# A decoder layer on one core: earlier fronts, reused tiles and one operand layout in an RWKV recurrence, and four residual adds moved through PSUM

## The chip, the cores and the metric

The kernel runs as one program on one core of a Trainium2 chip. The metric is the device time of one execution in microseconds (us). All tensors are float32.

## The reference, cut to what matters

One layer of a trunk, sequence 1024, width 1024. One projection of the normalised input feeds three things: an RWKV-7 branch, an S5 branch and two gates. The branches are gated, merged, projected and added to the input; a gated feed-forward block follows.

```python
def step(S, inp):                       # per head, 64x64 state
    r_t, w_t, k_t, v_t, a_t, b_t = inp  # a = -kk, b = kk * sigmoid(..)
    sa = jnp.einsum('bhij,bhj->bhi', S, a_t)
    S = S * w_t[:, :, None, :] + sa[..., None] * b_t[:, :, None, :] \
        + v_t[..., None] * k_t[:, :, None, :]
    return S, jnp.einsum('bhij,bhj->bhi', S, r_t)
y = group_norm(y) * lnx_w + lnx_b       # over each head
y = (y + sum(r * k * r_k) * v) * g
mixed = (g_rwkv * o_rwkv + g_s5 * o_s5) @ w_out
x = x + rms_norm(mixed, norm_mix_post)
x = x + rms_norm(conv_ffn(rms_norm(x, norm_ffn_pre)), norm_ffn_post)
```

## The kernel before, in words

Data lies with channels on the partitions and 512 time steps (a half, `th`) in a row. A product of float32 operands is made of three matmuls of split operands (high by high, low by high, high by low), at L179, L180 and L181 in the first half of the program; their outputs are the tiles `gm`, `ch` and so on. Weights are loaded by SP into `wf` (two buffers), cast to a high part `wh` by ACT (L159) and a low part `wl` by DVE (L160), four buffers each.

**The recurrence** is cut into four groups i = 0 to 3: a group is four heads (`g` = i % 2, as two pairs u = 0 and 1 of two heads on 128 partitions) over one half of the time (`th` = i // 2). A group goes through these functions:

- `rwkv_front` (L679), once per pair: loads k, tz, ta and r into tiles `ld` (ten buffers, L696), makes the norm of k with matmuls (L706), an inverse square root on DVE, a scan (L712), exponentials on ACT (L716, L717), the operands `ar` (L723, L732) and `bk` (L724, L735), and the products G of the two (L746), masked by DVE (L748) into `gr`. L727 copies the norm into `yb` for the transposes L729.
- `rwkv_inv` (L792): 62 small DVE operations (L805, L807) that invert triangles, fed and read back through DRAM by POOL.
- `rwkv_nat` (L764): transposes. `rwkv_level` (L819): joins the inverse's blocks with 32x32 matmuls (L832, L834) and ACT copies (L833, L835).
- `rwkv_chain` (L847): eight dependent chunks of 64 time steps that carry the state S, each with matmuls L880, L862, L891, L893, L898, L903 and, between them, short DVE and ACT operations (L883, L894, L895, L905, L866).
- `rwkv_out` (L917): group norm (L936 to L946), transposes (L952), scale and bias on ACT (L954), and two DVE operations (L957) with `bv` and `TG`, loaded through SP; the result goes to DRAM (`YR`).

**The order** of the instructions is written when the program is built, by `drive` (L203). It keeps an estimated clock `now` and runs generators ("lanes"): the chain lane (L2013), which takes the groups in order through nat, out of the group before, level and chain; two preparation lanes (L1991), one per pair, for front and inverse; and one for the S5 gate. When no lane is ready, it emits a step of the "fill": the gate products, the S5 products and the merge, independent work of three matmuls a piece. A lane gives with each `yield` how long it is not to be called again: T_KN after the front's first part, T_BK before G, T_INV for the inverse, T_LN for the norm. These constants, and conditions on counters, set where everything stands in each engine's queue. A queue is worked off in order on the chip.

In the preparation lane the front of group i may start once `nat` of group i - 1 is out. While it stands before `merge_s5`'s gates and the fourth chain is not done (`pause`), no fill is emitted.

**The end**: after the last product of the down projection, a sum of squares (`sumsq`, L263), an inverse root, a broadcast (`spread`, L289), and for eight tiles y = f * gain * bc (L1794) and y + residual (`add`, L1702), both on DVE, then one DMA each through SP (L1796).

## Time and profile before

| | |
|---|---|
| Median of 3 runs | 1569.41 us (1565.72 to 1578.88) |
| The profiled execution's own time | 1572.7 us |
| Its span | 1570.7 us |
| Mean granted TensorE clock | 0.964 of full speed |
| PE busy | 1488.5 us (95%) |
| DVE busy | 1164.0 us (74%) |
| ACT busy | 732.1 us (47%) |
| DMA | 224.46 MB, 143 GB/s |

The page's second part cuts the span in 40 slices of 39.3 us; a digit is the busy share in tenths, and PEclk is the clock that TensorE was granted. PE's busy time is not all useful: at a lower clock the same matmul is busy for longer, so that a stretch is read by busy time and clock together. The recurrence lies between about 275 and 814 us.

### The profile page before, as it was taken

The numbers are of one execution on the slowest core, as the hardware profiler recorded it, in microseconds if no ns is written. First come the engines' busy times: TensorE is split into PE (matmuls) and PEld (weight loads), VectorE is DVE, ScalarE is ACT, GpSimd is POOL, SyncE is SP. The second block draws the span as 40 slices with busy tenths as digits, with TensorE's granted clock in tenths as the row PEclk, the third lists the DMA queues.
The fourth block names the chain that finished last, engine by engine and source line by source line (L and its number), as shares of the span: only waits on it lengthen the run. The fifth ranks groups of instructions, "written<-read, shape, count | busy, mean of one in ns | idle before, by whom it ended". The sixth has DMA issues, their size and how long they took to land. (4 is left out here: it accounts for less than half of the span.)

```text
span 1570.7 us, 23456 instructions
## 1 busy us (share of the span) xinstructions
PE 1488.5 (95%) x8606; PEld 1193.9 (76%) x8606; DVE 1164.0 (74%) x2132; ACT 732.1 (47%) x1206; POOL 181.4 (12%) x340
## 2 busy tenths in 40 slices
PE   7997999999999989799799999999999999999995
PEld 5786888878676667577578788788888887788784
DVE  8878975747365569786467869788888887698777
ACT  6354434332344365257534556455555555443451
POOL 0022110123221121303100011000000000000000
PEclk9998999999998999899789999999999999999997
DMA  6454344443333174425325676233333335943722
GB/s 212 122 149 130 97 139 127 155 134 102 104 118 122 55 252 150 128 75 177 120 81 187 203 246 203 95 121 111 111 110 111 121 114 201 333 163 121 241 68 107
DMA packets 121123, 224.46 MB, mean 143 GB/s; under 512 B 30976, under 2 KB 37120, under 8 KB 121008
## 3 DMA queue, kind: packets, MB, share of 16 engines
q1 hardware_dynamic: 90144, 154.02, 30.9%
q0 software_dynamic: 21024, 64.71, 12.3%
q10 hardware_dynamic: 9840, 4.24, 1.0%
q8 instruction: 67, 1.10, 0.3%
q14 instruction: 48, 0.39, 0.1%
HBM read 163.41 MB, written 57.41 MB: 141 GB/s over the span
## 5 line engine op out<-in xcount | busy, mean ns | idle before, releaser
L179 PE MATMUL gm<-hh,wh 128*128 128x512 f32 x688 | 289.6, 421 | 6.9 <-ACT hh L244 6.2
L180 PE MATMUL gm<-hl,wh 128*128 128x512 f32 x688 | 273.7, 398 | 2.7 <-DVE hl L245 2.6
L181 PE MATMUL gm<-hh,wl 128*128 128x512 f32 x688 | 272.5, 396 | 0.0
L159 ACT CAST wh<-wf 128x512 fp32r<-128x512 f32 x178 | 109.9, 620 | 182.0 <-PE gm L180 111.6
L160 DVE TENSOR_TENSOR wl<-wf,wh 128x512 fp32r<-128x512 f32 x178 | 122.8, 693 | 73.1 <-ACT wh L159 71.9
L179 PEld LDWEIGHTS gm<-hh,wh 128*128 128x128 f32 x688 | 131.4, 191 | 41.3 <-ACT hh L244 9.1
L180 PEld LDWEIGHTS gm<-hl,wh 128*128 128x128 f32 x688 | 131.9, 192 | 28.8 <-DVE hl L245 6.2
L181 PEld LDWEIGHTS gm<-hh,wl 128*128 128x128 f32 x688 | 131.5, 191 | 28.6
L1751 PE MATMUL d<-xl,wh 128*128 128x512 f32 x308 | 120.5, 391 | 4.9 <-DVE xl L245 4.9
L1750 PE MATMUL d<-xh,wh 128*128 128x512 f32 x308 | 120.3, 391 | 0.3 <-DVE p L1702 0.3
L1752 PE MATMUL d<-xh,wl 128*128 128x512 f32 x308 | 119.9, 389 | 0.0
L1573 PE MATMUL rp<-t,h 128*128 128x512 f32 x252 | 98.3, 390 | 2.1 <-ACT p L1587 2.1
L1575 PE MATMUL rp<-t,l 128*128 128x512 f32 x252 | 98.1, 389 | 0.0
L1574 PE MATMUL rp<-t,h 128*128 128x512 f32 x252 | 98.0, 389 | 0.0
L1751 PEld LDWEIGHTS d<-xl,wh 128*128 128x128 f32 x308 | 57.8, 188 | 18.8 <-DVE xl L245 7.1
L244 ACT CAST h<-r 128x1024 fp32r<-128x1024 f32 (+1 forms) x40 | 34.0, 849 | 73.1 <-PE rp L1574 64.3
L1750 PEld LDWEIGHTS d<-xh,wh 128*128 128x128 f32 x308 | 57.8, 188 | 12.9 <-issue 0.7
L245 DVE TENSOR_TENSOR l<-r,h 128x1024 fp32r<-128x1024 f32 (+1 forms) x40 | 38.9, 972 | 38.5 <-ACT h L244 38.5
L1752 PEld LDWEIGHTS d<-xh,wl 128*128 128x128 f32 x308 | 57.8, 188 | 12.0
L1594 DVE SCALAR_TENSOR_TENSOR y<-zv,vecs,y 128x1023 f32<-128x1023 f32 (+1 forms) x42 | 53.8, 1282 | 10.2 <-ACT y L1592 10.2
L1573 PEld LDWEIGHTS rp<-t,h 128*128 128x128 f32 x252 | 47.3, 188 | 12.7 <-ACT p L1587 2.9
L1574 PEld LDWEIGHTS rp<-t,h 128*128 128x128 f32 x252 | 47.3, 188 | 9.8
(460 smaller groups left out, 3374.7 us busy)
## 6 DMA issues: line engine op xcount, KB each, us to landing
r<-in_w_up_dram SPq DMA_DIRECT2D x42, 512.0 KB, 3.6
wf<-in_w_in_dram SPq DMA_DIRECT2D x72, 256.0 KB, 3.1
st<-in_w_down_dram SPq DMA_DIRECT2D x55, 256.0 KB, 4.5
st<-ACT SPq DMA_DIRECT2D x44, 256.0 KB, 4.2
ACT<-y POOLq DMA_DIRECT2D x21, 512.0 KB, 2.9
GT<-ev POOLq DMA_DIRECT2D x32, 256.0 KB, 3.5
wf<-in_w_br_dram SPq DMA_DIRECT2D x32, 256.0 KB, 3.4
wf<-in_w_out_dram SPq DMA_DIRECT2D x32, 256.0 KB, 2.9
```

Of the source, the lines that this page charges most:

```text
L159: self.last_wh = nc.scalar.copy(h[:, :n], f[:, :n])
L160: low = nc.vector.tensor_tensor(l[:, :n], f[:, :n], h[:, :n].bitcast(F32), ALU.subtract)
L179: mm(ps, a, xh[k], start=a0, stop=False)
L180: mm(ps, a, xl[k], start=False, stop=False)
L181: mm(ps, b, xh[k], start=False, stop=z0)
L1573: mm(ps, wh[:, c], xh, start=first and k == 0, stop=False, skip_group_check=True)
L1574: mm(ps, wh[:, c], xl, start=False, stop=False, skip_group_check=True)
L1575: mm(ps, wl[:, c], xh, start=False, stop=k == 3, skip_group_check=True)
L1594: V.scalar_tensor_tensor(y[:, lag:], z[:, 0:1024 - lag], self.vec(nme, i), y[:, lag:], ALU.mult, ALU.add)
L1750: mm(ps, wh[:, c], xh[:, x], start=start, stop=False, skip_group_check=True)
L1751: mm(ps, wh[:, c], xl[:, x], start=False, stop=False, skip_group_check=True)
L1752: mm(ps, wl[:, c], xh[:, x], start=False, stop=stop, skip_group_check=True)
```

## The change

1. **Fronts earlier.** A preparation lane starts group i's loads once the chain of group i - 2 is out (`chains`); a second condition, after the wait T_LD, holds the front's other work until `nat` of i - 1 and `out` of i - 2 are out. `ar` and `bk` are allocated there.
2. **Operands alike.** In `ar` both heads of a pair have a in columns 0 to 63 and r in 64 to 127, so that `ar0` and `ar1` are one DVE operation of 128 partitions each where two of 64 were. `tk` lies in `yb` (a part of `gr`) and no longer in a tile `ld`, and the product r * r_k * tk is made in the front's first part.
3. **Outputs in loaded tiles.** `rwkv_out` loads `bv` and `TG` before the wait T_LN, most of them into the chain's spent `ar`; two DVE operations that take scale and bias from vectors replace the ACT operation and the two DVE operations. `rwkv_level` uses the inverse's spare tile `x` where it can.
4. **The planner's constants**: T_KN 17 to 12, T_BK 13 to 10, T_INV 62 to 58.
5. **The end.** The residuals of tiles 4 to 7 go into PSUM by a matmul with the identity (`resid_sum`), two before the sum of squares and two behind it; after L1794's operation a second identity matmul adds y, ACT copies the sum out, and DVE makes only four of the eight adds. The tiles are written in place.

The core of the diff (renamed slices left out):

```diff
     def rwkv_tiles(self, d, g, th):
         d.update(g=g, th=th)
-        pool = self.rk if g else self.rka
-        d["ar"] = self.tg("ar", 1, (128, 2, 8, 128), pool=pool)
-        d["bk"] = self.tg("bk", 1, (128, 2, 8, 128), pool=self.rka)
-        d["gr"] = self.tg("gr", 1, (128, 2, 8, 2, 128), pool=pool)
+        d["gr"] = self.tg("gr", 1, (128, 2, 8, 2, 128), pool=self.rk if g else self.rka)
         d["v"] = {}
         d["pt"] = self.tg("pt", 2, (128, 8, 2))
         d["md"] = self.dram.tile([2, 2, 16, 32, 32], F32, tag="md", name=self.nm("md"), bufs=3)
         d["bv"] = self.dram.tile([2, 128, 512], F32, tag="bv", name=self.nm("bv"), bufs=3)
-    def rwkv_front(self, d, u):
+    def rwkv_operands(self, d):
+        d["ar"] = self.tg("ar", 1, (128, 2, 8, 128), pool=self.rk if d["g"] else self.rka)
+        d["bk"] = self.tg("bk", 1, (128, 2, 8, 128), pool=self.rka)
+
+    def rwkv_front(self, d, u, i):
         nc, V, G, A = self.nc, self.nc.vector, self.nc.gpsimd, self.nc.scalar
         mm = nc.tensor.matmul
         o = slice(d["th"] * 512, d["th"] * 512 + 512)
         p = 2 * d["g"] + u
-        ar, bk = d["ar"][:, u], d["bk"][:, u]
-        ar0, ar1, bk0, bk1 = [[x[HS[h], :, HS[h ^ j]] for h in range(2)] for x in (ar, bk) for j in range(2)]
-
         gf = d["gr"][:, u].rearrange("p c h t -> p (c h t)")
         kk, yb, pe = gf[:, 0:512], gf[:, 512:1024], gf[:, 1024:1544].rearrange("p (c t) -> p c t", t=65)
...
         yield 0, T_LD
+        yield 0, lambda: self.nat >= i - 1 and self.outs >= i - 1
+        if "ar" not in d:
+            self.rwkv_operands(d)
+        ar, bk = d["ar"][:, u], d["bk"][:, u]
+        ar0, ar1 = ar[:, :, 0:64], ar[:, :, 64:128]
+        bk0, bk1 = [[bk[HS[h], :, HS[h ^ j]] for h in range(2)] for j in range(2)]
...
         A.activation(pe[:, :, 1:65], c64(tz), AF.Exp, scale=-0.5 * CDEC)
         A.activation(tz, tz, AF.Exp, scale=0.5 * CDEC)
         G.tensor_copy(d["pt"][:, :, u], pe[:, :, 64])
-        tk = self.tg("ld", NLD)
+        tk = yb
         A.activation(tk, ta, AF.Identity, bias=self.ka_1[:, p:p + 1], scale=self.ka_h[:, p:p + 1])
         V.tensor_tensor(tk, tk, k, ALU.mult)
+        V.tensor_tensor(ar1, c64(r), pe[:, :, 1:65], ALU.mult)
         for h, sl in enumerate(HS):
-            V.tensor_tensor(ar1[h], c64(r)[sl], pe[sl, :, 1:65], ALU.mult)
             V.tensor_tensor(bk1[h], c64(tk)[sl], c64(tz)[sl], ALU.mult)
+        V.scalar_tensor_tensor(r, r, self.vec("r_k", p), tk, ALU.mult, ALU.mult)
         yield 0.9, T_KN, 1.5
         kb = self.rp()
         A.copy(c64(yb), y.unsqueeze(2).to_broadcast([128, 8, 64]))
         for tb in range(4):
             nc.tensor.transpose(kb[:, tb * 128:(tb + 1) * 128], yb[:, tb * 128:(tb + 1) * 128], self.cst("ident"))
         V.scalar_tensor_tensor(kk, k, self.vec("k_k", p), kb, ALU.mult, ALU.mult)
-        for h, sl in enumerate(HS):
-            V.scalar_tensor_tensor(ar0[h], c64(kk)[sl], -1.0, pe[sl, :, 0:64], ALU.mult, ALU.mult)
+        V.scalar_tensor_tensor(ar0, c64(kk), -1.0, pe[:, :, 0:64], ALU.mult, ALU.mult)
         V.scalar_tensor_tensor(kk, ta, 1.0, kk, ALU.add, ALU.mult)
         for h, sl in enumerate(HS):
             V.scalar_tensor_tensor(bk0[h], c64(kk)[sl], 0.5, c64(tz)[sl], ALU.mult, ALU.mult)
         v = ld(self.RKV[8 + p], G)
         yield 0.5, T_BK
-        gm = [self.cst("gmask")[:, x].unsqueeze(1).to_broadcast([128, 4, 128]) for x in (slice(0, 128), slice(64, 192))]
+        gm = self.cst("gmask").unsqueeze(1).to_broadcast([128, 4, 128])
...
         for blk in range(2):
...
-                nc.gpsimd.dma_start(md[h], d["gr"][sl, u, :, h, sl])
-
-        V.scalar_tensor_tensor(r, r, self.vec("r_k", p), tk, ALU.mult, ALU.mult)
+                nc.gpsimd.dma_start(md[h], d["gr"][sl, u, :, h, 32 * blk:32 * blk + 32])
+
         pb = self.rp()
         mm(pb, self.cst("ones_bd"), r, start=True, stop=True)
...
+                    nc.gpsimd.dma_start(d["gr"][sl, u, :, h, 32 * blk:32 * blk + 32], xd[h])
+
...
         p0, p1 = [p0[:, u] for u in range(2)], [self.chb().rearrange("p (c t) -> p c t", t=32) for u in range(2)]
-        xz = self.tg("ld", NLD).rearrange("p (u c t) -> p u c t", u=2, t=32)
+        xz = (self.tg("x", 1, pool=self.rka) if spare else self.tg("ld", NLD)).rearrange("p (u c t) -> p u c t", u=2, t=32)
...
         o = slice(th * 512, th * 512 + 512)
         final = th == 1 and d["g"] == 1
-        ts = []
+        free = d["ar"].rearrange("p u c t -> p (u c t)").rearrange("p (j t) -> p j t", t=512)
         def factors(u):
             r = []
-            for src in (d["bv"][u], self.TG[2 * d["g"] + u][:, o]):
-                t = self.tg("ld", NLD)
+            for j, src in enumerate((d["bv"][u], self.TG[2 * d["g"] + u][:, o])):
+                t = self.tg("ld", NLD) if final or d["g"] > j else free[:, (2 if u == 0 else 0) + j]
                 (G if final else nc.sync).dma_start(t, src)
                 r.append(t)
             return r
         V.tensor_tensor(yn, yn, mean.unsqueeze(2).to_broadcast([128, 16, 64]), ALU.subtract)
         var = self.small.tile([128, 16], F32, tag="lv", name=self.nm("lv"), bufs=2)
         for j in range(2):
-            sq = self.tg("ld", NLD, (128, 8, 64))
+            sq = free[:, j].rearrange("p (a i) -> p a i", i=64)
             A.activation(sq, yn[:, 8 * j:8 * j + 8], AF.Square)
             V.tensor_reduce(var[:, 8 * j:8 * j + 8], sq, AX.X, ALU.add)
         V.tensor_scalar(var, var, 1.0 / 64, 64e-5, ALU.mult, ALU.add)
         y = self.rsqrt(var, 16, "or")
         V.tensor_tensor(yn, yn, y.unsqueeze(2).to_broadcast([128, 16, 64]), ALU.mult)
+        if not final:
+            ts = [factors(u) for u in range(2)]
         yield 0, T_LF if final else T_LN
         for u in range(2):
             p = 2 * d["g"] + u
             ps = self.rp((128, 4, 128))
             for c in range(4):
                 nc.tensor.transpose(ps[:, c], d["yn"][:, c, u], self.cst("ident"))
-            y1 = self.tg("ld", NLD)
-            A.activation(y1, ps.rearrange("p c t -> p (c t)"), AF.Identity, bias=self.vec("lnx_b", p),
-                         scale=self.vec("lnx_w", p))
-            for t, op in zip(ts[u] if final else factors(u), (ALU.add, ALU.mult)):
-                V.tensor_tensor(y1, y1, t, op)
+            y1, tg = ts[u]
+            V.scalar_tensor_tensor(y1, ps.rearrange("p c t -> p (c t)"), self.vec("lnx_w", p), y1, ALU.mult, ALU.add)
+            V.scalar_tensor_tensor(y1, y1, self.vec("lnx_b", p), tg, ALU.add, ALU.mult)
             if final:
                 self.br[p] = self.pair(1, p)
...
                     xs.append(x)
             return xs
-        def outputs(th, src, bc, xs):
+        def outputs(th, src, bc, xs, sums={}):
             for m in OUTORD[th]:
-                y = stage(0)[:, 0:512]
+                y = src[m] if th else stage(0)[:, 0:512]
                 V.scalar_tensor_tensor(y, src[m], self.vec("g_ffn_post", m), bc, ALU.mult, ALU.mult)
-                add(y, y, xs[m])
+                if m in sums:
+                    mm(sums[m], self.cst("ident"), y, start=False, stop=True)
+                    A.copy(y, sums[m])
+                else:
...
-        ss = bank(2)
+        ss, sums = bank(2), {}
+
+        def resid_sum(m, b):
+            sums[m] = bank(b)
+            mm(sums[m], self.cst("ident"), d["xs1"][m], start=True, stop=False)
+        resid_sum(4, 0)
+        resid_sum(5, 1)
         self.sumsq(ss, last[0], True)
         self.sumsq(ss, acc[1], False)
+        for m, b in ((6, 4), (7, 5)):
+            resid_sum(m, b)
         y = self.rstd(ss, 1e-6, 1.0 / D)
         bc = bank(3)
         self.spread(bc, y)
-        outputs(1, f[1], bc, d["xs1"])
+        outputs(1, f[1], bc, d["xs1"], sums)
     def build(self):
...
         for i, d in enumerate(self.ds):
-            yield 0, lambda: self.nat >= i - 1
+            yield 0, lambda: self.chains >= i - 1
             if not d:
                 self.rwkv_tiles(d, i % 2, i // 2)
-            yield from self.rwkv_front(d, u)
+            yield from self.rwkv_front(d, u, i)
             self.fronts += 1
...
             self.leveling = True
-            yield from self.rwkv_level(d)
+            yield from self.rwkv_level(d, i < 3 and self.prep == i)
             self.leveling = False
             yield from self.rwkv_chain(d)
+            self.chains = i + 1
             if i == 3:
                 self.pause, self.chained = False, True
...
 NEVA = 4
-T_KN, T_BK, T_GR, T_INV, T_LV, T_CH, T_LN, T_LF = 17.0, 13.0, 2.5, 62.0, 1.0, 0.8, 16.0, 14.5
```

The change moves the recurrence to other places in the queues. Three places follow.

PE, inside the fourth group's chain (`chk`, `chb` are the chain's PSUM tiles, `gm` those of the fill). Before, the last six chunks follow one another:

```order
L880 MATMUL chk_7890<-S_2603,ar_5878 64x64 x2
L862 MATMUL chk_7890<-UV_7357,gr_5880 64x64 x2
L880 MATMUL chk_7890<-S_2603,ar_5878 64x64 x2
L862 MATMUL chk_7890<-UV_7357,gr_5880 64x64 x2
L891 MATMUL chb_7891<-p_1498_7827,gr_5880 64x64 x4
L893 MATMUL chk_7890<-S_2603,ar_5878 64x64 x4
L898 MATMUL chk_7890<-UV_7357,gr_5880 64x64 x4
L903 MATMUL chb_7891<-UV_7357,bkn_7356 64x64 x4
L880 MATMUL chk_7928<-S_2603,ar_5878 64x64 x2
L862 MATMUL chk_7928<-UV_7357,gr_5880 64x64 x2
```

After, each chunk has six pieces of fill (18 matmuls) between its parts:

```order
L179 MATMUL gm_7470<-hh_6958,wh_7458 128x512
L180 MATMUL gm_7470<-hl_6959,wh_7458 128x512
L181 MATMUL gm_7470<-hh_6958,wl_7459 128x512
L179 MATMUL gm_7470<-hh_7042,wh_7464 128x512
L180 MATMUL gm_7470<-hl_7043,wh_7464 128x512
L181 MATMUL gm_7470<-hh_7042,wl_7465 128x512
L896 MATMUL chb_7493<-p_1388_7429,gr_5590 64x64 x4
L898 MATMUL chk_7492<-S_2603,ar_5731 64x64 x4
L179 MATMUL gm_7470<-hh_7096,wh_7464 128x512
L180 MATMUL gm_7470<-hl_7097,wh_7464 128x512
L181 MATMUL gm_7470<-hh_7096,wl_7465 128x512
L179 MATMUL gm_7470<-hh_7177,wh_7464 128x512
```

The fill that stood ahead of the chain now stands in it.

ACT, where the second group's level (`gr_3358` before, `gr_3026` after) meets the third group's front (`gr_4743`, `gr_4530`). Before:

```order
L700 ACTIVATE gr_4743<-ld_4747,vecs 128x512
L159 CAST wh_5039<-wf_5041 128x512
L1118 ACTIVATE ev_4802<-gm_4771,hb_b_gate 128x512
L720 ACTIVATE ld_4929<-ld_4751,ka_554,ka_h 128x512
L700 ACTIVATE gr_4743<-ld_4756,vecs 128x512
L716 ACTIVATE gr_4743<-ld_4749 128x8x64
L716 ACTIVATE gr_4743<-ld_4758 128x8x64
L717 ACTIVATE ld_4749<-ld_4749 128x512
L833 COPY ld_4793<-chb_4791 32x256 x2
L717 ACTIVATE ld_4758<-ld_4758 128x512
```

After:

```order
L159 CAST wh_4855<-wf_4857 128x512
L1123 ACTIVATE ev_4642<-gm_4555,hb_b_gate 128x512
L837 COPY x_4639<-chb_4637 32x256 x2
L837 COPY x_4639<-chb_4638 32x256 x2
L1123 ACTIVATE ev_4780<-gm_4657,hb_b_gate 128x512
L159 CAST wh_5105<-wf_5107 128x512
L732 COPY gr_4530<-rsy_4701 128x512
L839 COPY gr_3026<-chk_4636 32x8x32 x2
```

The front's casts of freshly loaded tiles (L700, L716, L717, L720) stood between the last chain and the level's copies L833; now they stand further ahead, and L837 (the former L833) follows a cast of weights and a gate.

DVE, where the fourth group's `bk` is made (L735 before, L739 after), on which its G matmuls wait. Before:

```order
L733 SCALAR_TENSOR_TENSOR gr_5880<-ld_5897,gr_5880 128x512
L1254 SCALAR_TENSOR_TENSOR hl_6334<-hl_6334,gm_6342 128x512
L160 TENSOR_TENSOR wl_6538<-wf_6539,wh_6537 128x512
L735 SCALAR_TENSOR_TENSOR bk_5879<-gr_5880,ld_5886 64x8x64
L735 SCALAR_TENSOR_TENSOR bk_5879<-gr_5880,ld_5895 64x8x64
L735 SCALAR_TENSOR_TENSOR bk_5879<-gr_5880,ld_5886 64x8x64
L735 SCALAR_TENSOR_TENSOR bk_5879<-gr_5880,ld_5895 64x8x64
L723 TENSOR_TENSOR ar_5878<-ld_5890,gr_5880 64x8x64
L1244 SCALAR_TENSOR_TENSOR ev_6307<-ev_6307,ev_6328 128x512
L756 SCALAR_TENSOR_TENSOR ld_5890<-ld_5890,vecs,ld_6034 128x512
L724 TENSOR_TENSOR bk_5879<-ld_6066,ld_5895 64x8x64
```

After:

```order
L1237 TENSOR_TENSOR hl_5933<-y_5929,hh_5932 128x512
L739 SCALAR_TENSOR_TENSOR bk_5732<-gr_5590,ld_5596 64x8x64
L1237 TENSOR_TENSOR hl_5940<-y_5936,hh_5939 128x512
L160 TENSOR_TENSOR wl_6056<-wf_6057,wh_6055 128x512
L1237 TENSOR_TENSOR hl_5947<-y_5943,hh_5946 128x512
L245 TENSOR_TENSOR hl_5951<-hl_5951,hh_5950 128x512
L245 TENSOR_TENSOR hl_5956<-hl_5956,hh_5955 128x512
L245 TENSOR_TENSOR hl_5961<-ld_5568,hh_5960 128x512
L160 TENSOR_TENSOR wl_6144<-wf_6145,wh_6143 128x512
L739 SCALAR_TENSOR_TENSOR bk_5732<-gr_5590,ld_5596 64x8x64
L245 TENSOR_TENSOR hl_5965<-ld_5571,hh_5964 128x512
L739 SCALAR_TENSOR_TENSOR bk_5732<-gr_5590,ld_5605 64x8x64
```

The S5 branch's four splits (L1232 before, L1237 after) stood 110 to 120 rows ahead of this place; now they, three splits of the RWKV values (L245) and two weight casts lie between the four operations on `bk`.

33 lines of the change are left out of this document (18 added, 15 removed).

## The prediction

> **What bounds the kernel now.** I read the page's slices first.
>
> ```profile
> PE   7997999999999989799799999999999999999995
> DVE  8878975747365569786467869788888887698777
> PEclk9998999999998999899789999999999999999997
> ```
>
> PE is full in nearly every slice; behind the start its dips lie in slices 15, 17 and 20 (39.3 us each), inside the recurrence, and at the end. So the kernel is bound by PE's work, and what this change can win is PE's lost time between 275 and 814 us and after the last product. The second view is PE by stages: length, then busy time and instructions of PE, PEld, DVE, ACT, POOL, then the granted clock, DMA's share and GB/s.
>
> ```profile
> 275.00:480.00 205.00, 203.70 (x1450) 157.83 (x1448) 120.61 (x336) 72.29 (x155) 50.65 (x89) 1.00 0.40 124
> 480.00:503.00 23.00, 20.25 (x178) 15.16 (x178) 13.88 (x40) 9.37 (x18) 2.71 (x5) 0.70 0.36 128
> 503.00:579.00 76.00, 75.02 (x704) 55.32 (x702) 40.05 (x96) 34.49 (x86) 15.70 (x30) 1.00 0.39 114
> 579.00:597.00 18.00, 11.36 (x35) 7.11 (x34) 15.63 (x36) 14.07 (x22) 2.13 (x4) 0.62 0.77 289
> 597.00:628.00 31.00, 30.80 (x140) 24.94 (x139) 29.41 (x88) 14.46 (x23) 5.27 (x9) 1.00 0.47 147
> 628.00:649.00 21.00, 11.51 (x58) 8.79 (x58) 17.61 (x28) 4.37 (x7) 6.93 (x12) 0.76 0.41 134
> 649.00:736.00 87.00, 85.90 (x833) 62.65 (x832) 61.85 (x165) 49.64 (x117) 17.61 (x32) 1.00 0.42 118
> 736.00:757.00 21.00, 15.37 (x174) 10.38 (x172) 11.26 (x16) 11.24 (x22) 2.14 (x4) 0.84 0.47 151
> 757.00:797.00 40.00, 31.66 (x420) 24.33 (x416) 17.43 (x44) 20.06 (x60) 4.79 (x9) 0.69 0.26 87
> 797.00:814.00 17.00, 17.00 (x79) 14.10 (x77) 13.20 (x41) 4.36 (x8) 0.00 (x0) 0.91 0.24 62
> 814.00:1549.00 735.00, 725.94 (x3235) 598.25 (x3233) 594.84 (x767) 365.92 (x500) 37.16 (x69) 1.00 0.47 158
> ```
>
> A stretch's work at full speed is about busy time by clock; the rest of its length is lost. A, 480 to 503: 23 - 20.25 x 0.70 = 8.8 us. B, 579 to 597: 18 - 11.36 x 0.62 = 11.0. C, 628 to 649: 21 - 11.51 x 0.76 = 12.3. D, 736 to 757: 21 - 15.37 x 0.84 = 8.1. The five other stretches up to 814 together lose 1.3 + 1.0 + 0.2 + 1.1 + 1.5 = 5.1. For E, 757 to 797, small dependent matmuls spoil that measure; I take the pace of a chain with fill instead (here L179's instructions alone: the first group's chain, then E; below them two starts four full-speed matmuls apart).
>
> ```profile
> 410.00:459.10 49.10, 20.60 (x47) 8.70 (x47) 1.00 0.30 87
> 757.00:797.00 40.00, 5.78 (x12) 2.37 (x13) 0.69 0.26 87
> 1526.68 0.39 PE L1752 MATMUL d<-xh,wl 128*128 128x512 f32 x1
> 1527.59 1.05 PE L289 MATMUL d<-csts,rsy 128*128 128x128 f32 x8
> ```
>
> A fill matmul is (1527.59 - 1526.68) / 4 = 0.228 us. The first chain holds 47 x 3 = 141 of them, 32.1 us, so its eight chunks cost PE (49.1 - 32.1) / 8 = 2.1 us each. E holds 36 (8.2 us) and eight chunks (17.0): 25.2 us of work in 40, a loss of 14.8. Behind 814 PE runs at clock 1.00 with 9 idle us in 735, so time won earlier should reach the end. All five losses: 8.8 + 11.0 + 12.3 + 8.1 + 14.8 = 55.0, with the rest 60.1 us. The third view says what PE waited for there (us, times, longest), and what ACT waited for in A and D.
>
> ```profile
> PE rp L746 <- DVE bk L724: 5.8, 1, 5.8
> PE chk L834 <- ACT gr L835: 5.6, 1, 5.6
> PE gm L179 <- ACT hh L244: 5.6, 3, 3.8
> PE rp L746 <- DVE bk L735: 3.9, 1, 3.9
> PE chk L834 <- ACT ld L833: 2.2, 1, 2.2
> ACT gr L700 <- DMA ld<-RKV: 3.7, 1, 3.7
> ACT wh L159 <- DMA wf<-in_w_glu_dram: 4.1, 1, 4.1
> ```
>
> C is front 3's G behind its `bk`, B the merge's first values behind ACT and DVE, A and D a level behind ACT's queue, where ACT itself waits for a load.
>
> **The change part by part.** *A: the third group's front.* Its loads move from behind out 0 to the middle of the first chain, and its ACT operations ahead of the level, so L833's follower no longer queues behind ACT's wait for `RKV`. What stays is a weight cast and a gate ahead of the copy. Bounds: 0, and the 3.7 us of that wait if loads are late again; I take 1.5.
>
> *E: the lone chain.* In the new order each of its chunks has 18 fill matmuls in it (4.1 us), so a chunk takes 4.1 + 2.1 = 6.2 us and loses no more than chain 1 did. Bounds: 0 and, if ACT's gelus and casts that now share the stretch pace the chunks, the 14.8 of before; I take 1.5, since the first chain kept that pace with DVE's and ACT's own work beside it.
>
> *B and C: DVE before the fourth front's G.* This is the part that eats the gain. G stood 168 fill matmuls later before. In the new order DVE must do the following between the second chain's end and G. The rows group DVE's operations between 520 and 645 us (busy, mean ns of one).
>
> ```profile
> L805 DVE TENSOR_TENSOR tm<-x,mt 128x120 f32<-128x120 f32 (+24 forms) x31 | 8.1, 260 | 0.3
> L732 DVE SCALAR_TENSOR_TENSOR ar<-gr 64x512 f32<-64x512 f32 x8 | 5.5, 686 | 0.2
> L1232 DVE TENSOR_TENSOR hl<-y,hh 128x512 fp32r<-128x512 f32 x4 | 4.2, 1057 | 0.1
> L245 DVE TENSOR_TENSOR hl<-hl,hh 128x512 fp32r<-128x512 f32 x2 | 1.4, 687 | 0.0
> L936 DVE TENSOR_REDUCE lm<-yn 128x16 f32<-128x1024 f32 x1 | 1.2, 1221 | 0.0
> L140 DVE TENSOR_TENSOR rsh<-rsy 128x8 f32<-128x8 f32 (+1 forms) x9 | 1.5, 170 | 0.1
> ```
>
> The third inverse: 62 x 0.26 = 16.1 us. Out 1: three passes of 1.22, six operations of 0.69 and some 12 of 0.17: 9.8. Front 3: 20 operations of 0.69 and 24 of 0.17: 17.9. Six weight casts of 0.69: 4.1. Four S5 splits of 1.06 and four value splits of 0.69: 7.0. Together 55 us. PE has in the same stretch 144 fill matmuls (32.8 us) and some 9 us of transposes and norms: 42. So DVE is 13 us late at G, less what it can start before the chain ends, plus PE's cold restart. The alike operands have already been counted: four operations of 0.69 fewer a group (L723 and L732, 64 partitions each, become one of 128; DVE's time goes with the 512 columns, as L732 and L245 show: 686 ns on 64 partitions, 687 on 128). The merge's first values are now split inside this stretch, so B's wait falls into it. B and C together then lose 13 where they lost 23.3. Bounds: 4, if only the last splits and casts stand in the way (row by row: three of L1237 and one of L245), and 23.3, unchanged. DVE full at 29.41 of 31 us from 597 on says the middle, 13.
>
> *D: level 3.* SP's order of stores and weight loads around out 2 is much as before, and ACT has three gelus ahead of L835's follower. Bounds 1 and 8.1; I take 4.
>
> *The planner's shorter waits.* Between the norm's matmuls and the transposes L729 PE emits 51 fill matmuls now (11.6 us); before it took 18.2:
>
> ```profile
> 352.85 1.84 PE L706 MATMUL rp<-csts,gr 128*128 128x2 f32 x16
> 363.30 1.14 ACT L727 COPY gr<-rsy 128x512 f32<-128x512 f32 x2 [9.20 <-DVE rsy L142]
> 371.01 0.60 PE L729 MATMUL rp<-csts,gr 128*128 128x128 f32 x4
> ```
>
> The copies were done at 364.4, 11.6 us after L706: the spare 6.6 us are all used, and no more. I leave the rest at 5 us, with 4 and 12 as its bounds.
>
> *Outputs in loaded tiles* take an ACT operation away and leave DVE's number, beside PE's fill: nothing here, except through the queues above; uncovered, one operation, 0.7 us a pair.
>
> *The end.*
>
> ```profile
> 1550.34 1.95 PE L263 MATMUL d<-ones,sq 128*128 128x1 f32 x16 [1.38 <-DVE sq L1702]
> 1554.71 2.07 PE L289 MATMUL d<-csts,rsy 128*128 128x128 f32 x8 [2.43 <-DVE rsy L142]
> 1556.83 1.41 DVE L1794 SCALAR_TENSOR_TENSOR st<-r,vecs,d 128x512 f32<-128x512 f32 x2 [2.17 <-PE d L289]
> 1558.15 1.29 DVE L1702 TENSOR_TENSOR st<-st,A 128x512 f32<-128x512 f32 x2
> L758 PE MATMUL rp<-ld,csts x16: 590/593/697, 316.0 to 660.1; 128*128 128x512 f32 x16
> ```
>
> Four adds of 0.6 (two start to end in 1.29) leave DVE: -2.4. An identity matmul is two instructions like L758's, about 1 us: the first two delay `sumsq` by 1549 + 2.0 - 1550.3 = 0.7; the second two hide under the 2.4 us of the root. They keep PE busy, so that L289 takes 1.05 as at 1527.59 and not 2.07: -1.0. The last four lie beside DVE. Sum -2.7. If PE has lost its clock by then, an identity matmul takes 2 us, the fourth copy comes 0.7 + 4 x 2 + 0.6 = 9.4 us after the broadcast, and four outputs wait behind it on SP: +1.5. Bounds -3.6 and +1.5; I take -2.7.
>
> In the Trainium skill, "TensorE: Matmul & The Clock Gate" (section "Part 1: The HAM clock gate") has it that the clock halves only after an idle window of about 3.4 us; by it the last four matmuls, 2 us behind the broadcast, stay fast and the end gives -2.7 as taken, while by the last stretch's low PE share alone it would be +1.5. The trace agrees only in part: the clock fell in C (0.76), behind a gap of 5.8 us, but L289 too took twice its time behind gaps of only 1.38 and 2.43 us with thin matmuls between them.
>
> **Sum.** Lost after: A 1.5, B and C 13, D 4, E 1.5, rest 5: 25.0. Won: 60.1 - 25.0 = 35.1, and 2.7 at the end: 37.8. From the profiled 1572.7 this is 1534.9; the median of the runs shown lies 3.3 lower, so 1531.6, rounded to 1531.
>
> **The rivals.** *DVE stays the bound*: B, C and D lose what they lost (31.4) and only A, E and the end are won: 7.3 + 13.3 + 2.7 = 23.3, time 1546. For it: DVE was at 15.63 of 18 us and 29.41 of 31 around B. Against: the same DVE work begins earlier, in a stretch where it was at 40.05 of 76.
> *PE never waits for DVE* because the inverse and front 3 start under the second chain: B and C 4, D 1, A 0: 13 us more, 1518. Against it the count of 55 above.
> *The fourth chain is still slow*, its chunks paced by ACT and not by 18 matmuls, so the change does not do what it says: E keeps its 14.8, time 1545. For it the gelus and casts that now stand in it; against it the first chain, at 2.1 us a chunk beside such work.
> *Slower: the shorter waits come too early.* One mechanism, at L729, L746 and the level of each front: the waits were cut by 6.6 us (measured), 3 and 4; if DVE needs all of them, PE stands for 13.6 us in each of four groups, in queue order, with all fill behind it: 54.4 us against 37.8 won, 1586. It decides from 37.8 / 4 = 9.5 us of new waiting a group. For it: at L729 the spare time is used to the last tenth. Against: 0 us were waited there before, and behind L729 most of the cut is filled by G's own operands.
>
> **How the numbers follow.** Forecast 0.50; DVE stays the bound 0.22; PE never waits 0.15; the fourth chain slow 0.08; slower 0.05. The low end is the second rival with the end at -3.6 and the rest at 4, 1516, and 2 us for the spread of runs: 1514. The high end is the first rival with E at 3, the rest at 7.5 and the end at +1.5: 1546 + 8.2 = 1554. A measurement of this kernel can tell about 1% (15.7 us) from no change: faster than 1553.7 are the forecast and three rivals, save their upper tails (0.07); so faster 0.88, same 0.07, slower 0.05.
>
> **What would show it.** In the changed profile: no lone chain at clock 0.5, chunks of the fourth chain 6.2 us apart; one PE wait of about 10 us or more for `bk` (L739) before G of the fourth front, and DVE full for some 50 us ahead of it; no wait of the second level for ACT above 2 us; L289 near 1.05 us at the end. It is wrong if G of the fourth front does not wait, if PE waits at L734 in every group, or if stretches behind the recurrence grow by what it wins.

## The result, and the profile after

| | before | after |
|---|---|---|
| Median | 1569.8 us (6 runs) | 1549.25 us (6 runs) |
| Range of the runs | 1565.72 to 1578.88 | 1542.4 to 1556.79 |
| The profiled execution, its span | 1572.7, 1570.7 | 1553.39, 1551.6 |
| Mean granted clock | 0.964 | 0.98 |
| PE busy | 1488.5 us | 1486.4 us |

The ratio of the times is 0.9858, with a 95% interval of [0.983, 0.9885]: 22 us less, at least 18 and at most 27. The forecast was 1531, some 38 us less. The direction and the range were right; a little over half of the gain came.

The slices of the page after, to be set beside those of before:

```profile
PE   7997999999999998989999999999999999999997
PEclk9998999999999999999999999999999999999999
```

The dip of slice 20 (the lone fourth chain) and the low clocks of slices 16, 17, 20 and 21 are gone (the first slice is number 1). Weak dips are left in slices 16 and 18 (a 9 became an 8), and the last slice went from 5 to 7. Next, PE by stages of the kernel after, with the columns of the stage table in the prediction. Lines moved by a few numbers: `bk` is now L739, G is L750, the level L836 and L838, the norm in `rwkv_out` ends with L951 and its transposes are L959.

```profile
275.00:454.00 179.00, 174.78 (x1280) 133.24 (x1279) 105.64 (x304) 57.16 (x125) 44.52 (x81) 0.98 0.43 127
454.00:487.00 33.00, 32.04 (x266) 24.63 (x266) 20.56 (x60) 18.97 (x42) 3.79 (x7) 0.90 0.29 97
487.00:542.00 55.00, 53.32 (x587) 37.43 (x586) 27.11 (x59) 19.73 (x58) 11.42 (x22) 1.00 0.45 126
542.00:585.00 43.00, 40.47 (x211) 32.83 (x209) 38.32 (x133) 23.54 (x43) 8.69 (x16) 1.00 0.42 129
585.00:619.00 34.00, 27.94 (x258) 20.13 (x258) 19.63 (x30) 12.28 (x24) 16.15 (x28) 0.90 0.61 176
619.00:672.00 53.00, 50.60 (x527) 35.70 (x527) 41.71 (x126) 27.07 (x72) 5.64 (x10) 1.00 0.51 145
672.00:712.00 40.00, 32.33 (x254) 24.12 (x253) 29.55 (x53) 23.83 (x46) 8.50 (x16) 0.87 0.43 139
712.00:763.00 51.00, 50.42 (x530) 35.57 (x529) 23.68 (x53) 28.91 (x75) 1.07 (x2) 1.00 0.26 75
763.00:791.00 28.00, 25.75 (x120) 21.24 (x120) 22.80 (x45) 14.49 (x26) 5.31 (x10) 0.99 0.58 191
```

Length less busy time by clock gives the losses as before; the clock is printed to two digits, so that the long first stretch is known to about 1 us and the others to 0.3. The third group's level (454 to 487): 33 - 32.04 x 0.90 = 4.2 us. The fourth front (542 to 619): 2.5 + 8.9 = 11.4. The third group's output and the fourth level (672 to 712): 40 - 32.33 x 0.87 = 11.9. The fourth chain (712 to 763): 0.6. The four other stretches: 7.7 + 1.7 + 2.4 + 2.5 = 14.3. Together 42.4 us, where before had 60.1 and the forecast 25.0.

What PE waits for between 250 and 810 us after (us in total, times, longest):

```profile
PE rp L750 <- DVE bk L739: 5.9, 2, 5.5
PE rp L959 <- DVE yn L951: 5.6, 1, 5.6
PE rp L750 <- DVE ld L762: 2.7, 3, 1.8
...
PE rp L263 <- DVE sq L1424: 2.3, 1, 2.3
PE gm L179 <- DVE last L1046: 2.0, 1, 2.0
PE rp L734 <- ACT gr L732: 1.8, 1, 1.8
```

The first wait was foreseen, at half its length. The second was not: PE stands before the transposes of the third group's output until DVE has finished that group's norm. The others are new and small.

The profiled execution was 4 us above its median. A second profile of the same kernel (label e12_change_again, below) has an own time of 1545.49 us. Its two longest waits are the same two, of 5.6 and 5.5 us. The stretches in question, and below them the first and the last of the recurrence:

```profile
542.00:585.00 43.00, 35.71 (x181) 28.95 (x179) 38.81 (x129) 23.50 (x40) 10.31 (x19) 0.99 0.47 144
585.00:619.00 34.00, 32.70 (x323) 23.62 (x323) 16.82 (x27) 8.76 (x20) 13.73 (x24) 0.92 0.66 183
672.00:712.00 40.00, 31.28 (x297) 22.78 (x295) 27.42 (x52) 23.71 (x47) 3.69 (x7) 0.96 0.40 141
275.00:454.00 179.00, 174.23 (x1287) 132.28 (x1287) 104.91 (x302) 61.84 (x135) 45.53 (x82) 0.99 0.42 124
763.00:791.00 28.00, 27.20 (x128) 22.46 (x127) 20.93 (x46) 10.83 (x20) 2.74 (x6) 1.00 0.66 225
```

It loses 7.6 + 3.9 = 11.5 us before the fourth front's end and 40 - 31.28 x 0.96 = 10.0 from 672 to 712, against 11.4 and 11.9. The stops belong to the kernel and not to one execution. The small losses do so only in part: the stretches outside the forecast's places lose 6.5 + 1.2 + 2.0 + 0.8 = 10.5 us here (the 1.2 and 2.0 from 487 to 542 and from 619 to 672) and 14.3 in the first profile.

### The profile page after: what moved, and what is told of

It reads as the page before. It is cut to its first block, busy times and chain, and to the rows that moved or that the text cites. A ratio compares the mean times of both kernels' runs of the same rounds, so it can differ in the third digit from the quotient of the medians.

```text
span 1551.6 us, 23464 instructions
## 1 busy us (share of the span) xinstructions
PE 1486.4 (96%) x8622; PEld 1186.8 (76%) x8622; DVE 1150.6 (74%) x2112; ACT 725.3 (47%) x1200; POOL 180.1 (12%) x340
## 4 chain that ended last, share of the span: by engine, by line
PE 71%; DVE 12%; DMA 7%; issue 5%; ACT 4%; SPq 0%; POOL 0%; DVEq 0%; ACTq 0%; POOLq 0%
PE gm L179 9%; PE gm L180 8%; PE gm L181 7%; PE rp L1578 5%; PE rp L1580 5%; PE rp L1579 5%; DMA st<-in_w_down_dram 2%; PE mm L1578 2%; PE mm L1580 2%; PE mm L1579 2%; PE ch L180 2%; PE ch L179 2%; PE ch L181 2%; PE mm L179 2%; PE mm L180 2%
## 5 line engine op out<-in xcount | busy, mean ns | idle before, releaser
L179 PE MATMUL gm<-hh,wh 128*128 128x512 f32 x688 | 292.6, 425 | 2.7 <-DVE last L1046 2.0
L160 DVE TENSOR_TENSOR wl<-wf,wh 128x512 fp32r<-128x512 f32 x178 | 122.5, 692 | 87.6 <-ACT wh L159 86.2
L179 PEld LDWEIGHTS gm<-hh,wh 128*128 128x128 f32 x688 | 131.7, 191 | 36.1 <-ACT spt L893 2.4
L1756 PEld LDWEIGHTS d<-xl,wh 128*128 128x128 f32 x308 | 57.8, 188 | 19.2 <-DVE xl L245 7.4
L245 DVE TENSOR_TENSOR l<-r,h 128x1024 fp32r<-128x1024 f32 (+1 forms) x40 | 38.9, 971 | 39.5 <-ACT h L244 39.4
L1757 PEld LDWEIGHTS d<-xh,wl 128*128 128x128 f32 x308 | 57.8, 188 | 11.9
L1578 PEld LDWEIGHTS rp<-t,h 128*128 128x128 f32 x252 | 47.3, 188 | 12.2 <-ACT p L1592 2.5
L1580 PEld LDWEIGHTS rp<-t,l 128*128 128x128 f32 x252 | 47.3, 188 | 9.9
```

The costliest lines, as they stand in the source:

```text
L160: low = nc.vector.tensor_tensor(l[:, :n], f[:, :n], h[:, :n].bitcast(F32), ALU.subtract)
L179: mm(ps, a, xh[k], start=a0, stop=False)
L1578: mm(ps, wh[:, c], xh, start=first and k == 0, stop=False, skip_group_check=True)
L1580: mm(ps, wl[:, c], xh, start=False, stop=k == 3, skip_group_check=True)
L1756: mm(ps, wh[:, c], xl[:, x], start=False, stop=False, skip_group_check=True)
L1757: mm(ps, wl[:, c], xh[:, x], start=False, stop=stop, skip_group_check=True)
```

## The experiments

The theory after the result: the gain comes from the places that the recurrence takes, above all from the fill inside the fourth chain, and the shortfall lies in two stops, before G of the fourth front and before the third output. The rivals: for the gain, that the cheaper operations earn part of it; for the first stop, that DVE's load decides (the forecast's reason); and that the stops' removal brings nothing, because the next instruction in order then waits. Ratios are to the kernel before on the same chip.

### Which part earned the gain

**The end alone (e1_new_end)**: the kernel before, with the change's end and nothing else.

```diff
-                add(y, y, xs[m])
+                if m in sums:
+                    mm(sums[m], self.cst("ident"), y, start=False, stop=True)
+                    A.copy(y, sums[m])
+                else:
+                    add(y, y, xs[m])
...
+        resid_sum(4, 0)
+        resid_sum(5, 1)
         self.sumsq(ss, last[0], True)
```

> The kernel before with the change's end alone (residuals of four tiles through PSUM, outputs in place). Theory of the prediction: L289 at its full pace (about 1.05 us) and four adds fewer on DVE, 2.7 us less than before. Rival: the identity matmuls run at half the clock and four outputs wait behind ACT's copies on SP, 1 to 2 us more than before.

Measured: 1569.27 beside 1571.28 us, 0.9977 [0.9956, 0.9998], -3.6 us (-6.9 to -0.3). The end's -2.7 lies well inside, and the rival's loss of 1 to 2 us is excluded.

**The old constants (e2_old_waits)** in the changed kernel:

```diff
-T_KN, T_BK, T_GR, T_INV, T_LV, T_CH, T_LN, T_LF = 12.0, 10.0, 2.5, 58.0, 1.0, 0.8, 16.0, 14.5
+T_KN, T_BK, T_GR, T_INV, T_LV, T_CH, T_LN, T_LF = 17.0, 13.0, 2.5, 62.0, 1.0, 0.8, 16.0, 14.5
```

> The change with the planner's old constants (T_KN 17, T_BK 13, T_INV 62). Theory A (DVE's queue is late at two places, G of the fourth front and the third group's norm): G stands 87 fill matmuls (20 us) later, so PE's wait for bk (5.9 us in the change's profile) is gone, and the last chunk of the fourth chain loses its fill (2 us): 0 to 6 us less than the change. Theory B (the cut waits are what cost): PE's waits in the fronts go in every group, 12 us or more less than the change. Theory C (the cut waits are what brought the chains together and so the gain): 8 us or more above the change.

Measured: 1552.96 us, 0.9881 [0.985, 0.9912]: 3.6 us above the change by the ratios, with overlapping intervals. None of the three theories said this.

**The old start of the fronts (e3_late_loads)** in the changed kernel:

```diff
-            yield 0, lambda: self.chains >= i - 1
+            yield 0, lambda: self.nat >= i - 1
```

> The change with the fronts' start put back to where nat of the group before is out (the rest of the change kept). Theory A: the third front's operations lie beside the second chain again, the wait before G of the fourth front shrinks by the 42 fill matmuls (9 us) that G moves back, and level 2 no longer meets the front: within 5 us of the change. Rival (the earlier start is what wins): 10 us or more above the change, near 1560.

Measured: 1556.96 us, 0.992 [0.9894, 0.9946]: 9.7 us above the change, so the rival was nearly right and theory A was not.

**Both old (e5_both_old)**: the two edits together; alike operands, reused tiles and the new end stay.

> The change with both the fronts' start and the three constants put back: its fronts, levels and chains stand at the same fill counts as before the change; what is left are the alike operands, the outputs in loaded tiles and the new end. If the moved places carry the gain in the recurrence, this is 1 to 6 us below the kernel before (the end's 2.7 to 3.6 us and little else), and the lone chain is back at half the clock. Rival (fewer and wider DVE operations and the freed tiles carry it): 10 us or more below the kernel before.

Measured: 1568.61 beside 1570.42 us, 0.9979 [0.9957, 1.0]. The fourth chain shows why. Three rows, one of a kernel each (old constants, old start, both), of L179's instructions alone while that chain runs:

```profile
727.90:782.80 54.90, 18.01 (x40) 7.57 (x40) 0.96 0.36 114
```

```profile
718.10:769.50 51.40, 20.52 (x46) 8.62 (x46) 1.00 0.34 99
```

```profile
761.20:800.40 39.20, 5.02 (x12) 2.12 (x12) 0.72 0.27 88
```

With one half of the moves undone the chain still has 40 or 46 pieces of fill in it; with both it has 12, as many as before, and clock 0.72. By the ratios, one half undone costs 3.6 us (constants) or 9.7 us (start), both 19: the moved places together carry nearly all of the gain. The chain's fill alone does not. With the old start the chain is as full as in the change, and yet 9.7 us are gone; what that profile shows elsewhere is a wait of PE before the fourth front's transposes, 1.8 us in the change and 5.3 with the old constants:

```profile
PE rp L734 <- ACT gr L732: 8.0, 1, 8.0
```

Whether that wait is the whole of the 9.7 us the runs do not show. What is left without the moves, 3.3 us, is what the end alone gave (3.6); alike operands and reused tiles, by themselves, earn nothing that these runs can tell.

### The stop before the fourth front's G

**Half the inverse (e6_half_inverse, e7_half_inverse_before)**: every second step left out, in the changed kernel and in the one before.

```diff
-        for q in range(31):
+        for q in range(0, 31, 2):
```

> The change with half of the inverse's steps left out (16 of 31 steps stay, so the inverse is not the reference's): some 30 DVE operations or 8 to 9 us of DVE less per group, and the order of all queues else as in the change. Theory A' (DVE's load is what holds PE, wherever the waits stand): PE's waits for DVE in the recurrence go and 10 to 16 us with them. Rival (latency between engines, PSUM buffers and POOL's transfers hold it, not DVE's load): within 4 us of the change.

> The kernel before with the same half of the inverse's steps left out. Theory A': C's two waits (9.7 us) shrink or go, but the lone chain and the level's waits for ACT stay: 6 to 12 us below the kernel before, less than the same cut brings in the change. Rival: within 4 us of the kernel before.

Measured: after, 1544.51 us, 0.9828 [0.9792, 0.9865]; before, 1569.7 us, 0.9988 [0.9967, 1.0009]. In the changed kernel the cut gives 4.7 us by the ratios, with overlapping intervals; before, nothing that the interval can tell, though PE's waits for `bk` there fall from 9.7 to 5.3 us. The two stretches with the fourth front in the changed kernel with the cut, and PE's wait in them:

```profile
542.00:585.00 43.00, 41.77 (x224) 34.16 (x223) 34.68 (x104) 21.43 (x39) 15.07 (x27) 1.00 0.46 135
585.00:619.00 34.00, 30.36 (x274) 20.91 (x274) 16.28 (x24) 12.35 (x25) 9.07 (x16) 0.80 0.60 181
```

```profile
PE rp L761 <- DVE gr L752: 3.0, 1, 3.0
```

From 542 to 598 DVE was busy for 47.53 of 56 us uncut and 44.82 with the cut. With less work the 5.5 us before `bk` are gone, but PE stands 3.0 us one step on, at the masks L752, and the two stretches lose 1.2 + 9.7 = 10.9 us where the change loses 11.4. That speaks against DVE's load as the whole of the bound; the time alone does not settle it, for the intervals leave room for the 10 us that this theory asked. What DVE waits for before the stop stands in the timeline of the kernel after (start, length, engine, line; in brackets how long the engine stood and who released it):

```profile
578.26 1.28 ACT L1229 ACT_TABLE_LOAD   x1 [3.99 <-DMA y<-YU]
...
581.75 1.10 DVE L1237 TENSOR_TENSOR hl<-y,hh 128x512 fp32r<-128x512 f32 x1 [2.22 <-ACT hh L1236]
...
590.45 0.69 DVE L739 SCALAR_TENSOR_TENSOR bk<-gr,ld 64x512 f32<-64x512 f32 x1
591.29 2.04 PE L750 MATMUL rp<-ar,bk 64*128 64x128 f32 x14 [5.54 <-DVE bk L739]
```

The merge's first values are loaded late (`YU`); ACT stands 4 us for them, then loads a table and makes gelu and cast; DVE stands 2.2 us for that cast; and the last `bk` stand behind the splits in DVE's queue. PE has passed all its fill by then. From 581.75 us to G's start DVE itself stands for only 0.27 us: there both its work and the order of it count.

**The front's operations ahead of the splits (e9_front_first)**: the merge's preparation gets a later place.

```diff
-                y = self.s5_y(y, b, 0)
-                self.xs0.append(self.pair(1, 4 + b))
-                self.s5_split(*self.xs0[b], y)
+                with self.tc.high_priority(HP - HPW):
+                    y = self.s5_y(y, b, 0)
+                    self.xs0.append(self.pair(1, 4 + b))
+                    self.s5_split(*self.xs0[b], y)
```

> The change with the merge's S5 loads, gelus, casts and splits ranked with the front and not above it: on DVE all four operations on the fourth front's bk (L739) then stand ahead of the four splits (L1237). Theory Q (G waits because bk stands behind splits in DVE's queue): PE's wait of 5.5 us for L739 goes and 5 us or more with it. Theory T (a break between two fills: the merge's operands use tiles that the last input products release, and between the two PE has little else to do): the wait for L739 goes but comes back as waits of the merge's first matmuls (L179, L180) for hh and hl, and the time is within 3 us of the change.

Measured: 1546.49 us, 0.9834 [0.9812, 0.9857]. The wait for `bk` is gone, and G waits at its next step:

```profile
PE rp L750 <- DVE gr L752: 3.5, 2, 3.3
```

Of this, 3.3 us lie before the fourth front's G. So the queue's order made the wait for `bk`, as the timeline says, but only 2 of its 5.5 us, and 3.8 us of time by the ratios (intervals overlap), are to be had from it, less than theory Q asked. Half the inverse less shortened the stop about as much, so the runs do not part order from load.

### The stop before the third output

**Room at both stops (e4_room)**: 8 us more ahead of the fourth G, 6 us more ahead of the third output.

```diff
-        yield 0.5, T_BK
+        yield 0.5, T_BK + (8.0 if i == 3 else 0)
...
+                if i == 3:
+                    yield 0, 6.0
```

> The change with 8 us more of the planner's time before G of the fourth front and 6 us more before the third group's out, both filled with fill matmuls. Theory A: both PE waits (5.5 us for bk L739, 5.6 us for yn L951) and the half clock behind them go, and nothing else is late: 8 to 12 us less than the change. Rival (DVE is full there, so the waits only move to the next place): within 3 us of the change, with other waits of the same size in the profile.

Measured: 1548.28 us, 0.985 [0.9817, 0.9883]. Both long waits are gone from the trace; the time is that of the change, as the rival said. In their place:

```profile
PE chk L885 <- DVE S L910: 4.9, 5, 2.0
PE chb L836 <- DVE x L833: 3.8, 2, 3.3
```

```profile
585.00:619.00 34.00, 28.57 (x256) 20.78 (x256) 18.46 (x28) 11.38 (x22) 10.57 (x18) 0.85 0.53 158
619.00:672.00 53.00, 48.19 (x471) 33.11 (x467) 35.48 (x97) 25.71 (x65) 7.22 (x13) 0.97 0.51 143
672.00:712.00 40.00, 37.84 (x311) 28.48 (x310) 33.72 (x82) 21.08 (x46) 11.97 (x21) 1.00 0.53 165
712.00:763.00 51.00, 48.18 (x515) 33.77 (x513) 24.66 (x51) 34.90 (x81) 1.61 (x3) 1.00 0.26 78
```

The stretch 672 to 712 now loses 2.2 us, but from 542 to 763 the five lose 2.5 + 9.7 + 6.3 + 2.2 + 2.8 = 23.5, against 2.5 + 8.9 + 2.4 + 11.9 + 0.6 = 26.3 in the change. The fill that is spent ahead of a stop is missing behind it: the third group's level waits for its transposes L833, and chunks wait for the state.

**Room at the third output alone (e10_out_room)**: the second of these edits.

> The change with 6 us more of the planner's time before the third group's out alone. The norm's transposes (L959) then find yn done: PE's wait of 5.6 us for L951 goes. If nothing behind it is late: 5 to 7 us less than the change. Rival (what is late is passed on to level 3 and the chain, as in the run with room at two places): within 3 us.

Measured: 1546.43 us, 0.983 [0.981, 0.985]: 4.4 us below the change by the ratios, with overlapping intervals, between the two expectations. Nine pieces of fill more stand ahead of the transposes, and PE still waits:

```profile
PE rp L959 <- DVE yn L951: 4.8, 1, 4.8
```

Why: DVE's groups in the kernel after from the norm's start to the transposes, 671.4 to 688.7 us, and the stretch's row:

```profile
L250 DVE SCALAR_TENSOR_TENSOR hl<-ev,hh 128x512 fp32r<-128x512 f32 x3 | 2.1, 690 | 0.4 <-ACT hh L249 0.4
L160 DVE TENSOR_TENSOR wl<-wf,wh 128x512 fp32r<-128x512 f32 x3 | 2.1, 685 | 0.2 <-ACT wh L159 0.2
L1264 DVE TENSOR_TENSOR ev<-ev,hl 128x512 f32<-128x512 f32 x3 | 2.1, 685 | 0.0
L1259 DVE SCALAR_TENSOR_TENSOR ev<-hl,gm 128x512 f32<-128x512 f32 x3 | 2.0, 683 | 0.4 <-PE gm L181 0.4
```

```profile
671.40:688.70 17.30, 11.36 (x68) 8.80 (x68) 15.75 (x34) 10.33 (x23) 8.57 (x16) 0.97 0.71 238
```

The merge's gates and splits (three each of L1264, L1259 and L250) and three casts of weights (L160), 8.3 us together, stand between the norm's own steps. They are DVE's part of the very fill that PE does meanwhile, so more fill ahead brings more of them: from its first reduction to the transposes the norm takes 17.1 us in the change and 22.5 us with the room (664.38 to 686.84). Before the change the third output stood later, beside other work:

```profile
715.00:727.00 12.00, 11.52 (x77) 9.25 (x73) 9.28 (x23) 9.58 (x23) 6.49 (x12) 1.00 0.41 119
```

There DVE had 9.28 us of work in 12, PE lost 0.5, and the norm took 11.4 us (715.62 to 727.05).

### The rest, and all together

**v loaded by SP (e8_v_on_sp)**, to see whether POOL's late load makes the waits for L762:

```diff
-        v = ld(self.RKV[8 + p], G)
+        v = ld(self.RKV[8 + p])
```

> The change with v loaded by SP and not by POOL, whose queue stands behind the inverse's transfers. If L762's wait for v is what delays the second half of G (PE's wait of 2.7 us for L762 in the change's profile, 2.3 of it at the second front), that wait goes and 2 to 6 us with it. Rival (L762 is late because of DVE's queue, not because of v): within 2 us, with the same wait in the profile.

Measured: 1545.61 us, 0.9847 [0.9818, 0.9877]; the wait for L762 is the same to the tenth (2.7 us, 3 times, 1.8). The load is not its cause. G of a pair's second half and L762's product use the same two PSUM buffers `rp`, which would explain it; that was not tried.

**Edits of e8, e9 and e10 together (e11_together)**:

> The change with three edits: the merge's S5 work ranked with the front, 6 us before the third group's out, v loaded by SP. If the waits that they remove are independent: 8 to 14 us less than the change, about 1538. Rival (the work that is late is the same whichever instruction waits for it): within 5 us of the change.

Measured: 1543.02 beside 1573.27 us, 0.981 [0.9787, 0.9834], some 7.5 us below the change by the ratios: between the two expectations. PE's longest waits left in it are 4.8 us for the third output's norm (L951), 3.7 for the masks L752 and 2.8 for the output L961.

**The change once more (e12_change_again)**:

> The change itself once more, for a second profile and a second interval. If its first profile is typical: PE waits again 5 to 6 us for L739 and for L951, loses about 7 us before the first chain that the kernel before does not lose, and the span is near 1551 us. If that profile was a long one: the two waits are there again, but the losses before the first chain are smaller, the third group's front is reached 5 us or more earlier and the span is below 1547 us. The ratio to the kernel before then lies near 0.984, and the three runs with one edit each are not shown to be better than the change.

Measured: 1548.74 us, 0.9857 [0.9831, 0.9882]; span of the profile 1543.7 us. The first profile was the longer one, but not by the losses ahead of the first chain: from 250 to 403 us this one loses 8.4 us and the first 7.8. It is 5.2 us ahead already when the first front's G starts (297.53 against 302.73 us), and still 5.2 at the third's. The three edits together (e11_together) are the fastest kernel of the study; their interval and this one just touch (0.9831 to 0.9834), so that this is likely and not shown.

## Why the prediction was half right, by its own steps

| loss in us | before | forecast | after | after, second profile |
|---|---|---|---|---|
| A, third front and level | 8.8 | 1.5 | 4.2 | 4.1 |
| B and C, merge's values and fourth front | 23.3 | 13 | 11.4 | 11.5 |
| D, fourth level, with the output ahead of it | 8.1 | 4 | 11.9 | 10.0 |
| E, fourth chain | 14.8 | 1.5 | 0.6 | 0.2 |
| the rest up to the chain's end | 5.1 | 5 | 14.3 | 10.5 |
| sum | 60.1 | 25.0 | 42.4 | 36.3 |

By the first profile 17.7 us were won there in place of 35.1. With 2.8 at the end and 1.3 us more lost just ahead (PE waits 2.0 us for L1046 in place of 0.7 for L720) this gives 19.2; the two profiled executions differ by 19.3. What was won did reach the end: behind the recurrence PE loses 9.1 us before (814 to 1549) and 8.7 after (791 to 1532).

- **The lone chain: right.** The fourth chain after, L179's instructions alone:

```profile
712.70:762.10 49.40, 20.58 (x47) 8.69 (x47) 1.00 0.26 75
```

47 x 3 fill matmuls are 32.1 us; the eight chunks take 6.2 us each and cost PE (49.4 - 32.1) / 8 = 2.2 us, against 2.1 in the first chain. By the table this place won 14.2 us, more than any other; that the moves as a whole carry the gain is shown (e5_both_old), that this place alone does is not.

- **The end: right.** The last product now ends at 1532.65 in a span of 1551.6, 18.9 us ahead of the end; before it was 21.7 us. From the timeline:

```profile
1536.08 1.96 PE L1868 MATMUL d<-A,csts 128*128 128x512 f32 x4
1538.64 1.16 PE L289 MATMUL d<-csts,rsy 128*128 128x128 f32 x8 [0.60 <-DVE rsy L142]
1540.64 3.70 PE L1801 MATMUL d<-r,csts 128*128 128x512 f32 x8 [0.84 <-DVE r L1799]
```

Two identity matmuls fill the root's time, L289 takes 1.16 and not 2.07, and the last four (eight instructions in 3.70) take 0.93 each, against the 1 us forecast at full pace. (In the bound of +1.5 the prediction adds 0.7 + 4 x 2 + 0.6 to 9.4; it is 9.3, which changes nothing.)

- **B and C: the size right, the reason only in part.** 13 forecast, 11.4 measured. But it rested on DVE full for 50 us and one wait of 10 us or more. The wait is 5.5 us, the restart at half pace behind it adds some 2, and the rest are smaller gaps; DVE itself stood 2.2 us for ACT, and half the inverse less moved the stop and hardly shortened the loss. Adding up DVE's work against PE's gave about the right number for a stop in which the order of a queue has a part: that the size came out is in part luck.

- **A: short by 2.7, and not by a wait.** The wait of the level for ACT is gone as forecast (PE waits there are 0.6 us and less), so the step on ACT's queue held. What is left is the clock. PE is busy without a gap from 467.0 to 479.6 us, and from 472.8 on its clock is half; the third row is the stage in e9_front_first, whose edit lies behind it:

```profile
467.00:472.80 5.80, 5.80 (x72) 4.55 (x71) 5.11 (x11) 0.87 (x3) 0.54 (x1) 1.00 0.52 181
472.80:479.60 6.80, 6.80 (x35) 5.32 (x35) 3.43 (x16) 1.41 (x3) 0.54 (x1) 0.50 0.01 4
454.00:487.00 33.00, 31.54 (x320) 23.94 (x318) 20.69 (x61) 18.23 (x42) 3.00 (x7) 1.00 0.34 113
```

  There the clock stays at 1.00 and the stage loses the forecast's 1.5 us; so it does in e8, e10 and e11 (0.8 to 1.5). Before the half clock stand the level's 32x32 matmuls (L836) and, moved beside them by the change, the third front's norm with 128x2 outputs (L710); that they are the cause was not tested. Before the change, too, only 2.8 of A's 8.8 us were idle time of PE and 6.1 were lost by the clock (0.70), which the forecast took for the queue's.

- **D: the step that failed.** The text costed the outputs at "beside PE's fill: nothing here" and looked only at level 3 behind ACT. It did not ask what else DVE would have to do at the output's new place. Moved 168 fill matmuls forward, the third output's norm fell among the merge's gates, and a norm that took 11.4 us in its old place took 17.1: PE stands for 5.6 us and restarts slowly. Forecast 4, measured 11.9 and 10.0.

- **The rest: the second step that failed.** "I leave the rest at 5 us" was not worked out from anything, though its upper bound was 12; it is 14.3 in one profile and 10.5 in the other. Part of it is the shortened waits: L750 waits up to 1.8 us for L762 in the second front, and never above 0.4 with the old constants. The rival "the shorter waits come too early" had the mechanism at a tenth of its size; its 13.6 us a group did not come, but its place L734 costs 8.0 us in one front once the fronts start late again (e3_late_loads). 2.3 us (L263 for L1424) are 0.8 in the second profile, and the causes of the others were not separated.

- **The rivals.** "DVE stays the bound" gave 1546, the number nearest to the measured 1549, but by another way: B and C shrank, and DVE's load was not the whole of the stop. The number does not speak for it. That PE never waits, and that the fourth chain stays slow, fell with the rows above.

What stays open: which of the remaining stops could be removed without making the next. The three tries at one or both of the long ones (e4_room, e9_front_first, e10_out_room) gave 1 to 5 us each by the ratios, inside the intervals.

## What to carry to other kernels

Where work is interleaved by hand, the gain of a move is read at the place that it leaves (here a chain without fill), but its cost at the place to which it goes: list what every in-order queue already holds there, evictions of the fill included, before calling an operation hidden. More fill ahead of a wait helps only if that fill does not load the engine that is waited for, and the fill comes out of what stands behind. And give the small remaining losses a worked-out term: here they made about as much of the shortfall (9.3 us, 5.5 in the second profile) as the long stop that was missed (7.9 and 6.0).

## What the runs showed of the hardware

PE's clock was full or half, and the price of a stop varied from one execution to the next. After the wait of 5.58 us for the third output's norm, the first row is the kernel after and the second its second profile, behind the same wait of 5.58 us:

```profile
688.70:694.30 5.60, 5.59 (x18) 4.73 (x19) 2.92 (x4) 0.20 (x1) 0.00 (x0) 0.50 0.23 90
683.30:686.10 2.80, 2.74 (x11) 2.58 (x12) 1.58 (x3) 0.00 (x0) 0.00 (x0) 0.50 0.00 0
```

PE is busy at a granted clock of 0.50 for 5.6 us in the one and 2.8 us in the other, so that 2.8 and 1.4 us are lost on top. In the Trainium skill, "TensorE: Matmul & The Clock Gate" (section "Part 1: The HAM clock gate") says that the array falls to half its clock after an idle window of about 3.4 us and needs about as long a busy one to come back, the windows running freely. The trace agrees with the two speeds, and a way back of 2.8 us here and 5.6 there fits windows that run freely. It does not agree that the fall takes an idle window: in A, above, the clock fell to 0.50 for 6.8 us while PE was busy for every one of the 5.8 us ahead (467.0 to 472.8), and in the second front it was 0.51 for the 3.4 us behind a wait of only 1.80 us (370.3 to 373.7).
